# A written issue table for VectorE, ScalarE, GpSimd and the load queue, from the ninth MLA step to the fourth Strassen block

## The chip, the cores and the metric

The kernel runs on one core of one Trainium2 chip. Its time is the device time of one execution in microseconds (us). The engines are TensorE (PE; its weight loader is listed as PEld), VectorE (DVE), ScalarE (ACT), GpSimd (POOL) and SyncE (SP), which issues most of the DMAs. [...]

## The reference

One layer of a hybrid encoder block, with 512 tokens, 1024 features and float32 throughout:

```python
h = rms_norm(x);  z = h @ w_in                      # all latents, q, k, v
y_mla  = mla_group(...)                             # 8 heads, qk 96 wide, v 64
y_diff = diff_group(...)                            # 4 heads, two softmaxes of 64 each, v 128
x = x + concat([y_mla, y_diff]) @ w_out
h2 = rms_norm(x)
x = x + (silu(causal_conv3(h2 @ w_gate)) * (h2 @ w_up)) @ w_down     # 2816 wide
x = x + sigmoid(rms_norm(x) @ w_pg) * (p @ w_pp)
```

Attention is block-causal in chunks of 64, so of four blocks of 128 queries the block t looks at (t + 1) * 128 keys.

## The kernel before, in words

**Three products for one.** Every large product is made of three TensorE products (`mm3`, L154 to L159): high part by high part, high by low, low by high. So each weight tile of 128x1024 and each activation half of 128x512 is split first: ScalarE casts it to the high part (`hi_d`, `hi_o`, `wAh`, `wSh`, `wTh`, `b1h`, `yh`, `st`, `ah`), and VectorE subtracts that from the source to get the low part (`lo_o`, `wAl`, `yh1l`, `al`; L151, L186, L189, L957). Until both parts are there, TensorE can't begin the products that read them.

**The stages of the stretch.** The program is one long sequence without a loop on the chip.

- MLA steps: four pairs of heads (hp) by four query blocks (t), `i = 4*hp + t`. A step makes logits on TensorE (`ml`), their row maximum on VectorE (L587, L590), the exponentials on ScalarE (`mla_exp`, L605), the division by the sums on VectorE (`mla_norm`, L614), transposes on TensorE (`pTm`, L547), a copy of the transposed tile out of PSUM on either engine (`probs_T`, L550 and L552), and the product with v (`mo`, L635). `pump` puts products of another stage (z columns `zd`, later `o`) between these steps, as filling for TensorE.
- Differential steps: four heads by four query blocks. Per step two logits (`dl`), their bias and row minimum on VectorE (L735), exponentials (L736), the combination of the two softmaxes (`diff_comb`, L744 to L746), transposes `pTd`, a ScalarE copy `pt` (L550) and the product `do` (L754). `diff_T` transposes q and k of the next head and splits them into `st` (L185 to L189). When a head is done, ScalarE squares and copies its result (`sqo` L760, `yd` L761). The filling is W_out: `hi_o` and `lo_o` split its tiles, the products go to `o`, and VectorE adds them to x (`add_x`, L684).
- The start of the feed-forward part: squares of x (L1008) and their sums on VectorE and GpSimd (L1010, L1012), the norm (`nr`, L1051), the products with w_pp (`pp`), which ScalarE copies out of PSUM (`ppo`, L1066) and SP stores (`pps`), the normed halves `xg` and their casts `b1h`, `b2h`.
- Feed-forward blocks of 128 gate and 128 up columns: three plain ones, then blocks by Strassen's seven products (`gu_units`), whose half-width products `gx` ScalarE copies out of PSUM (L1198 to L1214), with sums of weight quarters on VectorE. `cv` is the convolution, `ah` and `al` its split result for W_down.

**What sets the order.** TensorE's order is as written, in one region over the whole program. VectorE, ScalarE and GpSimd have regions of their own (`tc.manual_schedule`), in which they too issue as the code is written: the first from the start to the second call of `diff_comb` (the end of the MLA steps), the second from the start of the feed-forward part to the fourth Strassen block. Between the two, over the differential steps and W_out, a scheduler places their instructions by its own estimates, bounded by holds such as `tc.issue_after(df["comb"].ins)`, which keep an instruction behind a named one. SP's order is the scheduler's throughout.

Of the kernel before, what the change touches and what calls it, by code (L numbers as in the profile page):

```python
# [15 lines left out]
ALU = mybir.AluOpType  # L16
# [47 lines left out]

UP_BANKS = ("lg", "tp", "tp", "ob")

def _bucket(rel):
# [20 lines left out]
def _f32(ap):  # L90
    return ap.bitcast(F32)
# [3 lines left out]
def hybrid_block(ctx: ExitStack, tc: tile.TileContext, a: dict, out: bass.AP):  # L95
    nc = tc.nc
    V, S, G, TE = nc.vector, nc.scalar, nc.gpsimd, nc.tensor
# [13 lines left out]
    def bank(tag, name):  # L111
        return pp_.tile([P, 512], F32, tag=tag, bufs={"acc": 2, "lg": 3, "tp": 2, "ob": 1}[tag], name=name)

    def tt(name, dtype=F32):
        return att.tile([P, T], dtype, tag="tt", bufs=16, name=name)
# [10 lines left out]
    def xn_tile(name):  # L126
        return keep.tile([P, D], F32, tag="xn", bufs=4, name=name)
# [4 lines left out]
    def th_tile(name):  # L132
        return wts.tile([P, T], F32R, tag="th", bufs=8, name=name), wts.tile([P, T], F32R, tag="tl", bufs=8, name=name + "l")
# [6 lines left out]
    def load_raw(src, n, name):  # L140
        raw = wp["rawpool"].tile([P, 1024], F32, tag="raw", bufs=wp["raw"], name=f"raw_{name}")
        nc.sync.dma_start(raw[:, :n], src)
        return raw

    def load_w(src, n, name, eng=None):

        raw = load_raw(src, n, name)
        hi = wp["pool"].tile([P, 1024], F32R, tag="hi", bufs=wp["w"], name=f"hi_{name}")
        lo = wp["pool"].tile([P, 1024], F32R, tag="lo", bufs=wp["w"], name=f"lo_{name}")
        S.copy(hi[:, :n], raw[:, :n])  # L150
        (eng or V).tensor_tensor(lo[:, :n], raw[:, :n], _f32(hi[:, :n]), op=ALU.subtract)  # L151
        return hi, lo

    def mm3(ps, blocks, first=True, last=True, again=False):  # L154
        n = len(blocks)
        for i, (xh, xl, wh, wl) in enumerate(blocks):
            TE.matmul(ps, xh, wh, start=first and i == 0, stop=False, skip_group_check=again)  # L157
            TE.matmul(ps, xh, wl, start=False, stop=False, skip_group_check=again)  # L158
            TE.matmul(ps, xl, wh, start=False, stop=last and i == n - 1, skip_group_check=again)  # L159
# [22 lines left out]
    def split(h_, l_, src, col=None, eng=None):  # L182

        if col is None:
            S.copy(h_, src)  # L185
            return (eng or V).tensor_tensor(l_, src, _f32(h_), op=ALU.subtract)  # L186
        else:
            S.activation(h_, src, AF.Identity, scale=col)
            return V.scalar_tensor_tensor(l_, src, col, _f32(h_), op0=ALU.mult, op1=ALU.subtract)  # L189

    tsl = [slice(t * P, (t + 1) * P) for t in range(NT)]

# [24 lines left out]
    region = tc.manual_schedule(engines={mybir.EngineType.DVE, mybir.EngineType.Activation, mybir.EngineType.Pool})  # L217
# [32 lines left out]
    for kq in range(4):  # L250
        raw = xn_tile(f"xT{kq}")
# [11 lines left out]
        for j in range(2):  # L263
            k = 2 * kq + j
            xs, ws = raw[:, j * T:j * T + T], slice(416 * j, 416 * j + 416)
            h_, l_ = th_tile(f"xh{k}")
# [60 lines left out]
    raw, ukv_ = load_raw(a["w_ukv"], 1024, "ukv"), []  # L327
    for c in range(2):
        h_, l_ = tt(f"ukvh{c}", F32R), tt(f"ukvl{c}", F32R)
# [70 lines left out]
    def z_flush():  # L400
        while zouts:
            zouts.pop(0)()
# [258 lines left out]
    yh, yl, df = [None] * 8, [None] * 8, {}  # L661
# [12 lines left out]
    def wo_blocks(k0, k1, b, w):  # L674

        c = [slice((k % 4) * 256 + (b % 2) * P, (k % 4) * 256 + (b % 2) * P + P) for k in range(k0, k1)]
        return [(w[0][:, c[i]], w[1][:, c[i]], yh[k0 + i], yl[k0 + i]) for i in range(k1 - k0)]
# [5 lines left out]
    def add_x(b, ps):  # L683
        V.tensor_tensor(xb(b), xb(b), ps, op=ALU.add)  # L684

    wo2, wo_first = {}, {}

    def wo_w(kq, dq):
        if (kq, dq) in wo_first:
            return wo_first.pop((kq, dq))  # L690
        return load_w(a["w_out"][kq, dq], 1024, f"o{kq}{dq}")

    def wo_units(kq, dqs, nk):

        for dq in dqs:
            w = wo_w(kq, dq)
            if kq == 0 and dq + 1 in dqs:
                with tc.issue_after(df["comb"].ins):
                    wo_first[0, dq + 1] = wo_w(0, dq + 1)
            if kq:  # L700
                wo2[dq] = w
            steps = [(b, k) for b in (2 * dq, 2 * dq + 1) for k in range(0, nk, 2)]
            if (kq, dq) == (0, 0):
                steps.sort(key=lambda s: s[1])
            ps = {}
            for b, k in steps:
                if k == 0:
                    ps[b] = bank("acc", f"o{kq}{b}")
                mm3(ps[b], wo_blocks(4 * kq + k, 4 * kq + k + 2, b, w), k == 0, k == nk - 2)
                if k == nk - 2:  # L710
                    add_x(b, ps[b])
                yield
# [130 lines left out]
    for hp in range(HP):  # L843
        for t in range(NT):
            i = NT * hp + t
            last = hp == HP - 1
            n = FILL_MLA[hp][t]
            if t:
                mla_norm(hp, t)
            if t < NT - 1:  # L850
                mla_logits(hp, t + 1)
            if t == 2:
                for c, (d, m) in enumerate(((diff_T, (0, 0)), (diff_T, (0, 1))) if last else ((mla_q, (2 * hp + 2,)), (mla_k, (2 * hp + 2,)))):
                    d(*m)
                    mla_exp(hp, t + 1, c)
            elif t < 2:
                for c in range(2):
                    mla_exp(hp, t + 1, c)
            else:
                pump()  # L860
                n -= 1
                if last:
                    diff_logits(0, 0)
                else:
                    mla_q(2 * hp + 3)
                    mla_k(2 * hp + 3)
            if t == 0:
                mla_norm(hp, t)
            for e in extra.get(i, ()):
                e()  # L870
            pump(n)
            for e in late.get(i, ()):
                e()
            mla_T(hp, t)
            z_flush()
            if i in pvs:
                mla_pv(*pvs[i])
            if t == 3 and not last:
                mla_logits(hp + 1, 0)
                for c in range(2):  # L880
                    mla_exp(hp + 1, 0, c)
# [6 lines left out]
    diff_T(1, 1)  # L888
    y_hl(2, ymn[2])
    diff_comb(0, 1)  # L890
    region.__exit__(None, None, None)
    pump()
    for i, (h, t) in enumerate(dslots):
        if i + 2 < len(dslots):
# [27 lines left out]
    pk = kvp.tile([P, 4, 1024], F32R, tag="kv", name="pk")  # L922
    for i, (src, name) in enumerate(((a["pT"], "pT"), (a["w_pp"][0], "pp0"))):
        raw = load_raw(src, 1024, name)
        S.copy(pk[:, 2 * i], raw)
        with tc.issue_after(df["scale"].ins):
            V.tensor_tensor(pk[:, 2 * i + 1], raw, _f32(pk[:, 2 * i]), op=ALU.subtract)
    ptw, wpp = (pk[:, 0], pk[:, 1]), [(pk[:, 2], pk[:, 3])]
    order = (0, 4, 1, 5, 2, 6, 3, 7)
    early = {}  # L930
# [32 lines left out]
    def behind_head(src, tag, name, bufs=1):  # L963

        h_, l_ = (ffn.tile([P, 1024], F32R, tag=tag + j, bufs=bufs, name=f"{tag}{j}{name}") for j in "hl")
        with tc.issue_after(df["copy"].ins):
            df["hi"] = S.copy(h_, src)
        with tc.issue_after(df["scale"].ins):
            df["lo"] = V.tensor_tensor(l_, src, _f32(h_), op=ALU.subtract)
        return h_, l_  # L970

    gu = lambda f, c0, c1: a["w_gu"][f][:, 512 * c0:512 * c1]
# [1 line left out]
    W = {0: {0: behind_head(raw_w(gu(0, 0, 2), "rA", 0, bufs=2), "wA", 0, bufs=2)}}  # L974
    wpp.append(behind_head(rpp, "wT", "pp1"))

    region = tc.manual_schedule(engines={mybir.EngineType.DVE, mybir.EngineType.Activation, mybir.EngineType.Pool})
    region.__enter__()
    nr_ = [ffn.tile([P, 1024], F32, tag="raw", bufs=2, name=f"nr{i}") for i in range(2)]
    nrm = {"ss": nr_[0][:, :T], "dg": nr_[0][:, T:], "r": nr_[1][:, :T]}  # L980

# [32 lines left out]
            V.tensor_tensor(nrm["ss"], nrm["ss"], half, op=ALU.add)  # L1014
            V.tensor_tensor(nrm["ss"], nrm["ss"], sq, op=ALU.add)

    held = ExitStack()
    for i in ("hi", "lo"):
        held.enter_context(tc.issue_after(df[i].ins))
    for b in order:  # L1020
        if b in early:
            ps = early[b]
            mm3(ps, wo_blocks(7, 8, b, wo2[b // 2]), False, True)
        else:
            ps = bank("tp" if b == 3 else "lg", f"o3{b}")
            mm3(ps, wo_blocks(6 if b < 4 else 4, 8, b, wo2[b // 2]), True, True)
        add_x(b, ps)
        sums_of(b)
        held.close()
    wts.release()  # L1030


# [335 lines left out]
    next(w5)  # L1368
    fill.append(down_units(*groups[0], range(2), dn0))
    next(g)  # L1370
    region.__exit__(None, None, None)
    held = tc.issue_after(W["last"].ins)
    held.__enter__()
    for _ in w5:
# [3 lines left out]
    for f in range(NPLAIN + 2, NF):  # L1378
# [13 lines left out]
        else:  # L1392
# [4 lines left out]
            for n, i in (("b1", 0), ("b2", 2)):  # L1397
                h_, l_ = (ffn2.tile([P, 2, 1024], F32R, tag=n + j, name=f"pg{n}{j}") for j in "hl")
# [58 lines left out]
    def pg_bank(b):  # L1457
        return bank("acc" if b % 4 < 2 else "tp", f"pg{b}")
# [26 lines left out]
    for b in range(4, NK - 1):  # L1485
        p = pg_bank(b)
        pg(b, p)
        ple_out(b, p)
    for c in (0, H2):
        p = pg_bank(NK - 1)  # L1490
# [81 lines left out]
```

## Time and profile before

| | |
|---|---|
| time, median of 3 runs | 641.84 us (641.34, 641.84, 641.89) |
| time of the profiled execution | 642.33 us |
| its span, first to last instruction | 640.6 us |
| mean granted TensorE clock | 0.998 |
| MLA logits `ml` on TensorE, first and last start | 70.4 to 143.1 us |
| differential logits `dl`, likewise | 150.1 to 205.4 us |
| W_out products `o`, likewise | 155.2 to 230.9 us |
| Strassen products `gx`, likewise | 276.4 to 543.6 us |

The profiled execution took 0.49 us more than the median of the runs, and 1.7 us of its time lie outside the span. Rows of the timeline have the start and the duration in us, the engine, the line, the operation, output and inputs, the shape; in square brackets stands how long the engine was idle ahead of the instruction and what released it. Rows of waits have the waiting instruction, what it waited for, the sum in us, how often, and the longest. A row with x3 at its end joins three instructions.

### The profile page before, as it was taken

How to read it: one execution, taken by the hardware profiler on the slowest of the kernel's cores; microseconds unless marked ns; L12 is line 12 of the kernel's file. 1: busy time of each engine (PE TensorE's matmuls, PEld its weight loads, DVE VectorE, ACT ScalarE, POOL GpSimd, SP SyncE). 2: the span in 40 equal slices, each digit the busy share in tenths (PEclk: the TensorE clock that was granted, in tenths of full speed). 3: DMA queues.
4: the chain of work that ended last, by engine and by line, in shares of the span. 5: the costliest groups of instructions: out<-in, count | busy, mean ns of one | idle time of the engine just before them, and what ended most of it. 6: DMA issues, size and time to landing. Idle time of an engine off the chain costs nothing.

```text
span 640.6 us, 10207 instructions
## 1 busy us (share of the span) xinstructions
PE 630.7 (98%) x3900; PEld 557.3 (87%) x3900; DVE 486.4 (76%) x870; ACT 360.0 (56%) x629; POOL 68.5 (11%) x94
## 2 busy tenths in 40 slices
PE   9999999999999999999999999999999999999997
PEld 9988888886777887889999999999999999988886
DVE  6889677887899678888976767676767676759844
ACT  7896476756667455656554554545454545637111
POOL 1524103030000140101000000010000000000000
PEclk9999999999999999999999999999999999999999
DMA  8351611330231447547865646564646453542021
GB/s 294 112 165 33 187 66 62 100 131 2 67 100 34 164 135 243 133 99 166 215 186 123 194 119 181 116 181 116 182 115 184 119 175 116 182 131 64 31 87 50
DMA packets 29912, 82.63 MB, mean 129 GB/s; under 512 B 3100, under 2 KB 4124, under 8 KB 29736
## 3 DMA queue, kind: packets, MB, share of 16 engines
q1 hardware_dynamic: 23816, 69.17, 32.7%
q0 software_dynamic: 5616, 12.33, 11.3%
q8 instruction: 31, 0.51, 0.3%
q10 hardware_dynamic: 432, 0.49, 0.2%
q14 instruction: 17, 0.14, 0.1%
HBM read 77.77 MB, written 5.52 MB: 130 GB/s over the span
## 4 chain that ended last, share of the span: by engine, by line
PE 86%; DVE 7%; ACT 3%; issue 2%; DMA 1%; ACTq 0%; DVEq 0%; SPq 0%
PE dn L157 6%; PE dn L158 6%; PE dn L159 6%; PE gx L159 4%; PE gx L158 4%; PE gx L157 4%; PE zd L157 3%; PE zd L159 3%; PE zd L158 3%; PE g L157 3%; PE g L158 3%; PE g L159 3%; PE pg L159 2%; PE pg L158 2%; PE pg L157 2%
## 5 line engine op out<-in xcount | busy, mean ns | idle before, releaser
L957 DVE TENSOR_TENSOR wSl<-rS,wSh 128x1024 fp32r<-128x1024 f32 x21 | 25.7, 1224 | 43.6 <-ACT wSh L953 43.4
L157 PE MATMUL dn<-ah,hi_dn 128*128 128x512 f32 x144 | 56.2, 391 | 0.0
L158 PE MATMUL dn<-al,hi_dn 128*128 128x512 f32 x144 | 56.2, 391 | 0.0
L159 PE MATMUL dn<-ah,lo_dn 128*128 128x512 f32 x144 | 56.0, 389 | 0.0
L1074 POOL DMA_DIRECT2D rS<-in_w_gu x19 | 22.7, 1194 | 250.1 <-DVE cv L1242 115.2
L953 ACT CAST wSh<-rS 128x1024 fp32r<-128x1024 f32 x21 | 22.0, 1047 | 35.9 <-PE gy L158 35.6
L157 PE MATMUL zd<-hi_d,xh 128*128 128x512 f32 x96 | 39.2, 409 | 0.0
L158 PE MATMUL zd<-lo_d,xh 128*128 128x512 f32 x96 | 37.5, 391 | 0.0
L957 DVE TENSOR_TENSOR wTl<-rA,wTh 128x1024 fp32r<-128x1024 f32 x19 | 23.3, 1225 | 15.2 <-ACT wTh L953 14.7
L684 DVE TENSOR_TENSOR x<-x,dn 128x512 f32<-128x512 f32 x44 | 29.8, 678 | 6.1 <-PE dn L159 6.1
L159 PEld LDWEIGHTS dn<-ah,lo_dn 128*128 128x128 f32 x144 | 27.0, 188 | 5.7
L157 PEld LDWEIGHTS dn<-ah,hi_dn 128*128 128x128 f32 x144 | 27.1, 188 | 5.1
L158 PEld LDWEIGHTS dn<-al,hi_dn 128*128 128x128 f32 x144 | 27.1, 188 | 5.0
L1245 ACT ACTIVATE cv<-cv 128x512 f32<-128x512 f32 x22 | 13.9, 630 | 23.9 <-DVE cv L1242 23.8
L957 DVE TENSOR_TENSOR wAl<-rA,wAh 128x1024 fp32r<-128x1024 f32 x21 | 25.5, 1217 | 2.2 <-ACT wAh L953 2.2
L157 PE MATMUL o<-yh,hi_o 128*128 128x512 f32 x64 | 26.8, 419 | 0.0
L157 PE MATMUL g<-b2h,wAh 128*128 128x256 f32 (+1 forms) x88 | 26.4, 300 | 0.4 <-ACT g L1198 0.2
L953 ACT CAST wAh<-rA 128x1024 fp32r<-128x1024 f32 x21 | 22.1, 1050 | 8.3 <-DMA rA<-in_w_gu 8.2
L158 PE MATMUL g<-b2l,wAh 128*128 128x256 f32 (+1 forms) x88 | 26.2, 297 | 0.0
L159 PE MATMUL g<-b2h,wAl 128*128 128x256 f32 (+1 forms) x88 | 26.2, 297 | 0.0
L736 ACT ACTIVATE pmd<-pmd,nmd 128x128 f32<-128x128 f32 (+3 forms) x32 | 17.9, 560 | 14.7 <-DVE nmd L735 14.7
L1465 ACT ACTIVATE sg<-sg 128x512 f32<-128x512 f32 (+1 forms) x9 | 5.3, 584 | 36.8 <-DVE sg L1464 36.8
(479 smaller groups left out, 2219.6 us busy)
## 6 DMA issues: line engine op xcount, KB each, us to landing
rA<-in_w_gu SPq DMA_DIRECT2D x22, 512.0 KB, 3.9
rS<-in_w_gu SPq DMA_DIRECT2D x22, 512.0 KB, 3.7
rS<-in_w_gu POOLq DMA_DIRECT2D x19, 512.0 KB, 6.1
raw_dn<-in_w_down SPq DMA_DIRECT2D x18, 512.0 KB, 5.8
raw_d<-in_w_d SPq DMA_DIRECT2D x12, 512.0 KB, 3.4
r<-in_w_gu SPq DMA_DIRECT2D x19, 256.0 KB, 5.9
raw_o<-in_w_out SPq DMA_DIRECT2D x8, 512.0 KB, 3.7
rS_pg<-in_w_pg SPq DMA_DIRECT2D x6, 512.0 KB, 4.0
```

Source lines behind the costliest of these rows:

```text
L157: TE.matmul(ps, xh, wh, start=first and i == 0, stop=False, skip_group_check=again)
L158: TE.matmul(ps, xh, wl, start=False, stop=False, skip_group_check=again)
L159: TE.matmul(ps, xl, wh, start=False, stop=last and i == n - 1, skip_group_check=again)
L684: V.tensor_tensor(xb(b), xb(b), ps, op=ALU.add)
L736: S.activation(pm[:, :n], pm[:, :n], AF.Exp, bias=nm, scale=-1.0, accum_out=s0 if m == 0 else s1)
L953: S.copy(h_, src)
L957: V.tensor_tensor(l_, src, _f32(h_), op=ALU.subtract)
L1074: nc.gpsimd.dma_start(sums[f].rearrange("p (i c) -> p i c", i=2), a["w_gu"][f][:, :2048].rearrange("p (i c) -> p i c", i=2)[:, :, :512], a ...
L1245: S.activation(cv, cv, AF.Silu)
L1465: S.activation(sg, sg, AF.Sigmoid)
```

## The change

TensorE's region stays as it is. The first region of the other engines now ends at the ninth MLA step (`i == 8`), where the position in the program is marked; the second region and all holds between are gone. At the place where the second region ended, `in_order(mark)` takes all instructions of VectorE (305), ScalarE (191), GpSimd (14) and SP (42) since the mark and chains each engine's in the order of a written table. Each link only orders two instructions of the same engine; no semaphore comes with it.

```diff
+ISSUE = {
+    mybir.EngineType.DVE: [
+        0, 7, 1, 2, 3, 4, 5, 8, 6, 36, 9, 10, 12, 11, 13, 14, 15, 17, 27, 28, 18, 19, 21, 23, 22, 24, 20, 25, 26, 16, 31, 33, 30, 37, 32, 47, 34, 35,
...
+    mybir.EngineType.SP: [
+        0, 5, 6, 7, 1, 2, 3, 4, 8, 9, 10, 11, 12, 13, 14, 15, 16, 20, 26, 27, 28, 34, 17, 18, 19, 29, 31, 21, 36, 22, 23, 24, 25, 39, 30, 33, 32, 37,
+        35, 40, 38, 41,
+    ],
+}
...
+    def traced():
+        return len(nc.cur_bb.bb.instructions)
+
+    def in_order(mark):
+
+        ins = nc.cur_bb.bb.instructions
+        for e, order in ISSUE.items():
+            x = [i for i in ins[:mark] if i.engine == e and type(i).__name__.startswith("Inst")][-1:]
+            y = [i for i in ins[mark:] if i.engine == e and type(i).__name__.startswith("Inst")]
+            assert sorted(order) == list(range(len(y)))
+            x += [y[k] for k in order]
+            for p, q in zip(x, x[1:]):
+                tc.add_manual_dep(q, p.name, mybir.DependencyInfo(mybir.DependencyClass.NoSync, mybir.DependencyReason.DATA), reason="issue order")
...
-                with tc.issue_after(df["comb"].ins):
-                    wo_first[0, dq + 1] = wo_w(0, dq + 1)
+                wo_first[0, dq + 1] = wo_w(0, dq + 1)
...
+            if i == 8:
+                region.__exit__(None, None, None)
+                mark = traced()
...
     diff_comb(0, 1)
-    region.__exit__(None, None, None)
...
-    region = tc.manual_schedule(engines={mybir.EngineType.DVE, mybir.EngineType.Activation, mybir.EngineType.Pool})
-    region.__enter__()
...
     next(g)
-    region.__exit__(None, None, None)
+    in_order(mark)
```

The left-out hunks remove the other holds (`df["copy"]`, `df["scale"]`, `df["hi"]`, `df["lo"]`). Both programs hold the same instructions with the same shapes and tiles; TensorE's 3760 and GpSimd's 99 rows stand in the same order in both. SP has two moves among its 164: one load of `rS` and one of the 128x512 weight tile `r` now each stand ahead of a load for W_down. The rest of the change is the order on VectorE and ScalarE. In the listings below a number behind a name marks one tile; tiles made later in the program have numbers lower by one or two after the change, and lines of the changed kernel are 32 to 46 higher.

VectorE at the turn from the MLA steps to the differential ones: `dl` are the first differential logits, `pTm` the last transposed MLA tiles, `yh1l` the low part of an MLA result, which only W_out reads. Before:

```order
L552 COPY pt<-pTm_1732 128x384
L613 RECIPROCAL sums<-sums 128x2
L614 TENSOR_SCALAR pm<-pm,sums 128x512 x2
L735 ISA pmd,nmd<-dl_1764,strip 128x128
L735 ISA nmd 128x1
L735 ISA pmd,nmd<-dl_1772,strip 128x128
L735 ISA nmd 128x1
L186 TENSOR_TENSOR yh1l<-ym_1425,yh_1780 128x512
L552 COPY pt<-pTm_1784 128x512
```

The same place after:

```order
L218 TENSOR_TENSOR yh1l<-ym_1426,yh_1781 128x512
L598 COPY pt<-pTm_1733 128x384
L659 RECIPROCAL sums<-sums 128x2
L660 TENSOR_SCALAR pm<-pm,sums 128x512 x2
L780 ISA pmd,nmd<-dl_1765,strip 128x128
L780 ISA nmd 128x1
L183 TENSOR_TENSOR lo_o_1973<-raw_o_1970,hi_o_1972 128x1024
L598 COPY pt<-pTm_1785 128x512
L780 ISA pmd,nmd<-dl_1773,strip 128x128
```

`yh1l` has moved from right ahead of the copy of `pTm_1784` to six rows earlier; in its place, two rows up, stands a low part of W_out, `lo_o`, and the copy has passed the second logits' `L735`.

ScalarE where the first differential head ends and the third one's q is split (`d0T_2083` into `st`). Before:

```order
L736 ACTIVATE pmd,s_1948<-pmd,nmd 128x384
L736 ACTIVATE pmd,s_2036<-pmd,nmd 128x384
L550 COPY pt<-pTd_2064 128x128
L150 CAST hi_o_2504<-raw_o_2502 128x1024
L760 ACTIVATE sqo<-do_1946 128x512
L761 COPY yd_2072<-do_1946 128x512
L188 ACTIVATE st<-d0T_2083,dcol 128x512
L736 ACTIVATE pmd,s_1948<-pmd,nmd 128x512
```

The same place after:

```order
L596 COPY pt<-pTd_2064 128x128
L781 ACTIVATE pmd,s_1948<-pmd,nmd 128x384
L805 ACTIVATE sqo<-do_1946 128x512
L806 COPY yd_2072<-do_1946 128x512
L220 ACTIVATE st<-d0T_2083,dcol 128x512
L781 ACTIVATE pmd,s_2036<-pmd,nmd 128x384
```

The cast `hi_o_2504` has gone from here. It now stands a whole step earlier on ScalarE, ahead of another copy of transposed probabilities:

```order
L781 ACTIVATE pmd,s_1867<-pmd,nmd 128x384
L182 CAST hi_o_2504<-raw_o_2502 128x1024
L596 COPY pt<-pTd_1941 128x256
L781 ACTIVATE pmd,s_1763<-pmd,nmd 128x512
L781 ACTIVATE pmd,s_1913<-pmd,nmd 128x512
```

ScalarE in the first Strassen blocks: the copy of `gx_3113` (3111 after) frees the PSUM bank for the next product. Before:

```order
L953 CAST wAh_3043<-rA_3041 128x1024
L1130 ACTIVATE bth<-xg_2851 128x512
L1131 CAST bth<-xg_2873 128x512
L953 CAST wTh_3059<-rA_3041 128x1024
L185 CAST ah_3063<-cv 128x512
L1198 COPY g_3114<-gx_3113 128x256
```

The same place after:

```order
L999 CAST wAh_3041<-rA_3039 128x1024
L1169 CAST bth<-xg_2856 128x512
L217 CAST ah_3020<-cv 128x512
L1169 CAST bth<-xg_2871 128x512
L999 CAST wTh_3057<-rA_3039 128x1024
L999 CAST wAh_3136<-rA_3134 128x1024
L1236 COPY g_3112<-gx_3111 128x256
```

The 128x512 cast of the convolution's result `ah_3063` (3061 after) has gone from ahead of the copy, and the next block's weight cast `wAh_3136` has come there.

More of the change, by code (lines that the diff above doesn't have):

```diff
@@ L65 @@
 UP_BANKS = ("lg", "tp", "tp", "ob")
+ISSUE = {
+    mybir.EngineType.DVE: [
[11 rows of a table added]
+    ],
+    mybir.EngineType.Activation: [
[6 rows of a table added]
+    ],
+    mybir.EngineType.Pool: [
+        0, 1, 2, 3, 4, 5, 6, 7, 8, 9, 10, 11, 12, 13,
+    ],
+    mybir.EngineType.SP: [
+        0, 5, 6, 7, 1, 2, 3, 4, 8, 9, 10, 11, 12, 13, 14, 15, 16, 20, 26, 27, 28, 34, 17, 18, 19, 29, 31, 21, 36, 22, 23, 24, 25, 39, 30, 33, 32, 37,
+        35, 40, 38, 41,
+    ],
+}
 def _bucket(rel):
@@ L925, in hybrid_block @@
         S.copy(pk[:, 2 * i], raw)
-        with tc.issue_after(df["scale"].ins):
-            V.tensor_tensor(pk[:, 2 * i + 1], raw, _f32(pk[:, 2 * i]), op=ALU.subtract)
+        V.tensor_tensor(pk[:, 2 * i + 1], raw, _f32(pk[:, 2 * i]), op=ALU.subtract)
     ptw, wpp = (pk[:, 0], pk[:, 1]), [(pk[:, 2], pk[:, 3])]
@@ L965, in behind_head @@
         h_, l_ = (ffn.tile([P, 1024], F32R, tag=tag + j, bufs=bufs, name=f"{tag}{j}{name}") for j in "hl")
[L966 to L969, printed above, removed]
+        S.copy(h_, src)
+        V.tensor_tensor(l_, src, _f32(h_), op=ALU.subtract)
         return h_, l_
@@ L1015, in sums_of @@
             V.tensor_tensor(nrm["ss"], nrm["ss"], sq, op=ALU.add)
-    held = ExitStack()
-    for i in ("hi", "lo"):
-        held.enter_context(tc.issue_after(df[i].ins))
     for b in order:
@@ L1028, in hybrid_block @@
         sums_of(b)
-        held.close()
     wts.release()
```

16 rows, old and new, of the table ISSUE are left out of this document.

## The prediction

> **What bounds the kernel now.** I read the page first, its span:
>
> ```profile
> span 640.6 us, 10207 instructions
> ```
>
> and the chain of work that ended last, by engine:
>
> ```profile
> PE 86%; DVE 7%; ACT 3%; issue 2%; DMA 1%; ACTq 0%; DVEq 0%; SPq 0%
> ```
>
> TensorE carries the chain. So the kernel gets shorter only where TensorE stands still, and the next view is the busy time by stretch: the stretch of the change, rounded outward, and the steady blocks behind it.
>
> ```profile
> 130.00:300.00 170.00, 165.84 (x992) 136.99 (x991) 139.02 (x295) 102.56 (x209) 18.70 (x13) 1.00 0.40 118
> 300.00:500.00 200.00, 200.00 (x1390) 187.54 (x1389) 148.77 (x202) 104.83 (x158) 16.68 (x14) 1.00 0.60 158
> ```
>
> The columns are length, then busy time of PE, PEld, DVE, ACT and POOL, then granted clock. From 130 to 300 us TensorE idles 170.00 - 165.84 = 4.16 us; from 300 to 500 us never. What the change wins before 300 us is therefore not given back by a queue behind it: TensorE is the bound there, and it only starts earlier. What TensorE waited for in the stretch, and three rows of its weight loader's waits that the first list does not have in full:
>
> ```profile
> PE mo L635 <- DVE pt L552: 0.7, 1, 0.7
> PE pTm L547 <- DVE pm L614: 0.6, 1, 0.6
> PE dl L159 <- DVE st L189: 0.6, 1, 0.6
> PE pTm L547 <- DVE st L186: 0.5, 1, 0.5
> PE g L157 <- ACT ppo L1066: 0.5, 1, 0.5
> PE pTd L547 <- ACT pt L550: 0.5, 1, 0.5
> PE g L157 <- ACT g L1198: 0.2, 1, 0.2
> ```
>
> ```profile
> PEld g L157 <- ACT g L1198: 1.0, 2, 0.7
> ...
> PEld gx L159 <- DVE wAl L957: 0.5, 2, 0.3
> ...
> PEld dl L157 <- ACT st L188: 0.3, 1, 0.3
> ```
>
> The seven waits make 3.6 us. They understate the loss, because a product's last part overlaps its follower: in the rows of 278.78 and 279.01 us below, products that are listed with 0.39 us start 0.23 us apart, so a stall costs its listed idle time and 0.16 us more. From below a wait costs its listed idle time, from above that and 0.16.
>
> **The change part by part.** TensorE's instructions, order and shapes are the same, so no work is added or removed on it. What changes is when the other engines' results come. I go through the listed waits.
>
> *pTm behind pm (0.6).* The division waits for row maxima that VectorE takes late:
>
> ```profile
> 134.41 0.28 PE L159 MATMUL ml<-st 100*128 100x128 f32 x1
> ```
>
> ```profile
> 135.08 0.41 DVE L590 TENSOR_REDUCE sums<-ml 128x2 f32<-128x256 f32 x1
> ```
>
> The logits end at 134.41 + 0.28 = 134.69, the maximum starts 0.39 later, behind two scalings of `zd` and a copy. In the table one of the two scalings has left that place. Gain at most 0.39 and at least 0; I take 0.30, as some hand-over remains. The remaining 0.3 or so of this wait is the chain itself.
>
> *pTm behind st (0.5).*
>
> ```profile
> 145.30 0.74 DVE L189 SCALAR_TENSOR_TENSOR st<-d0T,dcol,st 128x512 fp32r<-128x512 f32 x1
> ...
> 146.44 0.69 DVE L186 TENSOR_TENSOR st<-d1T,st 128x512 fp32r<-128x512 f32 x1 [0.40 <-ACT st L185]
> ```
>
> The second split waits 0.40 for a ScalarE cast, which stood behind an exponential there. The table puts both casts ahead of the exponentials and takes a reduction from between the two VectorE splits, so the second follows the first at about 145.96 (145.30 + 0.74, less the 0.08 by which such operations overlap): 0.48 earlier. The bounds are 0.4 (the idle time shown) and 0.5 + 0.16; I take 0.48.
>
> *mo behind pt (0.7).*
>
> ```profile
> 152.39 0.69 DVE L186 TENSOR_TENSOR yh1l<-ym,yh 128x512 fp32r<-128x512 f32 x1 [1.24 <-ACT yh L185]
> 153.00 0.68 DVE L552 COPY pt<-pTm 128x512 f32<-128x512 f32 x1
> ```
>
> `yh1l`, wanted only by W_out, held the copy back for 153.00 - 152.39 = 0.61. It moves away; in its place comes a `lo_o`, 1.22 long by its like at 197.06 below, but ahead of it VectorE idled 1.24. Gain 0.60; 0 if that `lo_o` starts late, 0.87 (0.7 + 0.16) if the copy may start earlier still. I take 0.60, since the 1.24 covers the 1.22 with nothing to spare.
>
> *dl behind st (0.6, and the loader's 0.3).* ScalarE ran a weight cast in front of the evictions of a finished head and the split behind them:
>
> ```profile
> 174.79 1.05 ACT L150 CAST hi_o<-raw_o 128x1024 fp32r<-128x1024 f32 x1
> ```
>
> Lost are 0.6 + 0.16 at this wait and, by the loader's row, 0.3 at the `dl` that waits for ScalarE's half: 1.0. The cast of 1.05 goes from this chain, and VectorE makes the low half of `st` one logit earlier. Gain 1.0; from below 0.6, the wait shown.
>
> *pTd behind pt (0.5).*
>
> ```profile
> 197.06 1.22 DVE L151 TENSOR_TENSOR lo_o<-raw_o,hi_o 128x1024 fp32r<-128x1024 f32 x1
> ```
>
> ```profile
> 199.94 0.40 ACT L736 ACTIVATE pmd<-pmd,nmd 128x128 f32<-128x128 f32 x1 [1.89 <-DVE nmd L735]
> ```
>
> ScalarE stood 1.89 for a VectorE minimum behind that `lo_o`, then did this exponential, then the copy. The table moves the `lo_o` behind other work and this exponential ahead of an earlier copy. Gain 0.55, between 0.40 (the exponential alone) and 0.66 (0.5 + 0.16).
>
> *g behind ppo (0.5).*
>
> ```profile
> 240.36 0.59 ACT L1051 COPY nr<-nrb 128x512 f32<-128x512 f32 x1 [2.98 <-PE nrb L1050]
> ...
> 244.33 0.58 ACT L1066 COPY ppo<-pp 128x512 f32<-128x512 f32 x1
> ```
>
> Lost: 0.5 + 0.16 = 0.66, behind the copy of 244.33, which like two others ran between the casts of the normed halves. Two of these copies move into the 2.98 us in which ScalarE had nothing to do. Gain 0.66, and 0 if the chain from the norm to the casts is late itself.
>
> *g behind g, gx behind wAl (0.2 in the first list, 1.0 and 0.5 in the loader's).*
>
> ```profile
> 277.75 1.05 ACT L953 CAST wTh<-rA 128x1024 fp32r<-128x1024 f32 x1
> 278.71 0.61 ACT L185 CAST ah<-cv 128x512 fp32r<-128x512 f32 x1
> 279.22 0.36 ACT L1198 COPY g<-gx 128x256 f32<-128x256 f32 x1
> ```
>
> ```profile
> 278.78 0.39 PE L158 MATMUL u<-b2l,wSh 128*128 128x512 f32 x1
> 279.01 0.39 PE L159 MATMUL u<-b2h,wSl 128*128 128x512 f32 x1
> 279.64 0.39 PE L157 MATMUL g<-b2h,wAh 128*128 128x256 f32 x1 [0.24 <-ACT g L1198]
> ```
>
> Lost here: 0.63 - 0.23 = 0.40; the like of it some 18 us later 0.3 (the loader's 1.0 less its longest, 0.7). The table takes `ah` away and sets `wTh` and the next `wAh` so far ahead that ScalarE waits for TensorE at the copy. The two `wAl` move right behind `wTl`: 0.4 of the loader's 0.5. Gain 0.40 + 0.3 + 0.4 = 1.1.
>
> [...]
>
> **What the moves cost.** Ten 1024-wide pieces of W_out (four `hi_o` at 1.05, six `lo_o` at 1.22, by their rows above; 11.5 us in all) stand at other places of the differential steps, among them three `hi_o` right in front of copies of `pTd`. ScalarE is busy 102.55 of 170.00 us, so mostly they fall into idle time; from below 0, from above three times 1.05. I take 0.5, half of one cast, since the stalls shown behind such a piece (0.6 behind the `hi_o` of 1.05, 0.5 behind the `lo_o` of 1.22) were about half of it.
>
> At the start of the feed-forward part a load is held back:
>
> ```profile
> 226.02 3.07 DVE L684 TENSOR_TENSOR x<-x,o 128x512 f32<-128x512 f32 x5
> ```
>
> ```profile
> 226.55 0.38 SPq L948 DMA_DIRECT2D r<-in_w_gu  x1
> ```
>
> ```profile
> r<-in_w_gu SPq DMA_DIRECT2D x19, 256.0 KB, 5.9
> ```
>
> SP's next `rS` load waits until VectorE has made w_pp's low part, which the table puts behind the additions to x: these end at 229.09, the low part (1.22) at 230.3, the load of `r` behind it goes out near 231.2 instead of 226.55 and lands 5.9 later, near 237.1. Its cast now stands between the second and third `ppo`, so ScalarE and all behind it wait for it; then three copies of some 0.5 end near 239.3, 1.1 ahead of the `nr` copy at 240.36. So I cost it at nothing; a landing over 1.1 us later would come through. The other load that SP takes earlier, ahead of one for W_down, has a consumer far behind the stretch and costs nothing.
>
> GpSimd's sums of squares now run beside w_pp's low part, whose two inputs lie in SBUF. The nearest row is a VectorE sum of two SBUF inputs that fell into a GpSimd sum:
>
> ```profile
> 227.44 4.38 POOL L1010 TENSOR_TENSOR nr<-nr,nsq 128x512 f32<-128x512 f32 x3 [9.90 <-ACT nsq L1008]
> ```
>
> ```profile
> 229.85 0.82 DVE L1012 TENSOR_TENSOR nr<-nr,nsq 128x512 f32<-128x512 f32 x1 [0.76 <-ACT nsq L1008]
> ```
>
> It took 0.82 against 0.69 for `yh1l` of the same shape at 152.39: 0.13 more. So I cost the overlap at 0.1, which lies off the path and adds nothing to the sum; bounds 0 and one GpSimd sum, 4.38 / 3 = 1.46. [...]
>
> **The sum.** 0.30 + 0.48 + 0.60 + 1.0 + 0.55 + 0.66 + 1.1 = 4.7, less 0.5 for new waits: 4.2. Against its own time the profiled execution would take 642.33 - 4.2 = 638.1; the median lies 0.49 below the profiled run, 641.84 - 4.2 = 637.6, say 637.7.
>
> **The rivals.**
> - *Half is given back.* A freed TensorE asks for everything earlier, and some results then come too late: a `hi_o` in front of a `pTd` copy shows in full at two of three places (2.1), or the overlap with GpSimd or the late `r` delays the norm (1.0 to 1.5). For it: the `lo_o` that replaces `yh1l` fits by 0.02 us. Against it: ScalarE and VectorE have 67 and 31 us idle between 130 and 300 us. Time: half the gain, 641.84 - 2.1 = 639.7.
> - *Nothing moves.* The waits sit in chains (logit, maximum, exponential, sum, division, transpose, copy) that are as long in any order, and each place that is eased shows the next engine's lateness. For it: two releasers are VectorE, two ScalarE in the same chains. Against it: the rows show at each place one instruction that isn't of the chain. Time 641.8.
> - *Slower.* One mechanism: the moved 1024-wide splits in the differential steps come to stand in front of `pTd` copies and minima that TensorE waits for. They hold 11.5 us; more than 4.7 + 1.3 = 6.0 of it, over half, must show on TensorE before the kernel is slower by 0.2%. With 7 it would take 641.84 + 7 - 4.7 = 644.1. Against it: before, the same ten were there as well, and cost some 1.5 (1.0 at `dl`, 0.55 at `pTd`).
>
> **How the numbers follow.** My forecast has 0.66, half given back 0.22, nothing 0.08, slower 0.04. The forecast's own ends are 636.7 (no new wait, 4.7, and 0.4 from the upper ends of the first and third place) and 638.9 (a sum of 2.9: the lower ends of the terms for `st`, `dl` and `pTd`, 0.4 + 0.6 + 0.40, in place of 2.03, and a whole cast shown, 1.05, and 0.1 of the overlap with GpSimd). The range takes in half given back with some more: 636.7 to 640.3. What a measurement of this kernel can tell from no change is about 0.2%, 1.3 us. Faster by more than that holds the first two cases: 0.88; within it 0.08; slower 0.04.
>
> **What would show it.** Right: in the changed kernel TensorE idles at most 1.5 us between 130 and 300 us, the waits for `st`, `pt` of L552, `ppo` and `g` are gone from its list, and each stage starts earlier by the sum so far (half a microsecond less from the `hi_o` on): the first `dl` by 0.8, the first plain block's `g` by 3.1, the steady blocks by 4.2 us. Wrong: a wait of `do` or `pTd` for `pt` behind a `hi_o`; `nr` no earlier than before; a gap ahead of the first `g` behind `r`; or idle time behind 300 us, since the order at the end of the stretch hands over to the scheduler.

## The result

The changed kernel takes 636.25 us (median of 6 runs, 635.92 to 637.34) against 641.95 us (6 runs, 641.34 to 643.64): a ratio of 0.991, 95% interval 0.9896 to 0.9923, or 5.7 us. Forecast were 637.7 and a range of 636.7 to 640.3, so it gained more than was forecast, and 0.45 us more than the range allowed. Its profiled execution took 635.92 us, 0.33 below its median. Of all runs reported here one, of the kernel with the new order in the second half only, took 1251.71 us; it is left out of that kernel's median.

The span and the chain that ended last, from the page of the changed kernel:

```profile
span 634.2 us, 10212 instructions
...
PE 98%; DMA 1%; DVE 1%; ACT 0%; issue 0%; ACTq 0%
```

VectorE and ScalarE, 10% of the chain before, have all but left it. The same two stretches as before (length, then busy time of PE, PEld, DVE, ACT and POOL), and all waits of TensorE that are listed in the first:

```profile
130.00:300.00 170.00, 169.37 (x1021) 141.39 (x1020) 143.55 (x302) 108.27 (x215) 16.91 (x13) 1.00 0.43 127
300.00:500.00 200.00, 200.00 (x1397) 187.90 (x1396) 145.46 (x197) 103.64 (x155) 15.50 (x13) 1.00 0.58 154
```

```profile
PE pTm L593 <- DVE pm L660: 0.3, 1, 0.3
PE mo L681 <- DVE pt L598: 0.2, 1, 0.2
```

TensorE idles 0.63 us where it idled 4.16, and of seven waits two are left. For `pm` the prediction had named a rest of 0.3; the one for `pt` (L552 before) it had expected to be gone, and 0.2 of it is left. Behind 300 us it still never idles.

TensorE issues the same products in the same order in both kernels, so one product's start before, less its start after, is the advance won up to there. The two profiled executions differ by 0.67 us already at 60 us, and still at 120 us; the first moved instruction runs at 114 us. That part is no effect of the change and is taken off here.

| product | start before | start after | advance, less 0.67 | step | the prediction's term |
|---|---|---|---|---|---|
| `pTm` behind `pm` | 137.43 | 136.43 | 0.33 | 0.33 | 0.30 |
| `pTm` behind `st` | 147.19 | 145.60 | 0.92 | 0.59 | 0.48 |
| `mo` behind `pt` | 153.74 | 151.64 | 1.43 | 0.51 | 0.60 |
| `dl`, third head, last product of the pair | 178.73 | 175.35 | 2.71 | 1.28 | 1.0 |
| `dl`, fourth head, last product of the pair | 195.39 | 191.73 | 2.99 | 0.28 | none |
| `pTd` behind `pt` | 200.85 | 196.67 | 3.51 | 0.52 | 0.55 |
| first `g` of the feed-forward part | 244.97 | 240.07 | 4.23 | 0.72 | 0.66 |
| second `g` product behind `gx`'s copy | 279.86 | 274.48 | 4.71 | 0.48 | 0.40 |
| `gx` product after that behind `wAl` | 283.27 | 277.60 | 5.00 | 0.29 | 0.2 |
| second `g` product of the next block | 298.30 | 291.89 | 5.74 | 0.74 | 0.5 |
| new waits | | | | 0 | -0.5 |

The steps make 5.74, and the medians differ by 5.70. The row of 279.86 holds three things: the wait for `gx`'s copy, 0.48; 0.16 more won at the products right behind the first `g`; and a loss of 0.17 at the second half of the first plain block, where a copy of `pp` stood 1.8 us behind a store. That loss is in this profile alone; the profiles of all runs below lack it, and without it the sum would be 5.9.

### The profile page after: what moved, and what is told of

Read it like the earlier page. It is cut to its first block, busy times and chain, and to the rows that moved or that the text cites. A ratio compares the mean times of both kernels' runs of the same rounds, so it can differ in the third digit from the quotient of the medians.

```text
span 634.2 us, 10212 instructions
## 1 busy us (share of the span) xinstructions
PE 627.6 (99%) x3900; PEld 555.7 (88%) x3900; DVE 485.3 (77%) x870; ACT 360.7 (57%) x629; POOL 69.7 (11%) x94
## 3 DMA queue, kind: packets, MB, share of 16 engines
q0 software_dynamic: 5616, 12.33, 11.5%
## 4 chain that ended last, share of the span: by engine, by line
PE 98%; DMA 1%; DVE 1%; ACT 0%; issue 0%; ACTq 0%
PE dn L189 6%; PE dn L190 6%; PE dn L191 6%; PE gx L191 4%; PE gx L190 4%; PE gx L189 4%; PE g L190 4%; PE g L191 4%; PE g L189 4%; PE zd L189 4%; PE zd L191 3%; PE zd L190 3%; PE o L189 3%; PE o L191 2%; PE u L189 2%; PE o L190 2%
## 5 line engine op out<-in xcount | busy, mean ns | idle before, releaser
L999 ACT CAST wTh<-rA 128x1024 fp32r<-128x1024 f32 x19 | 20.0, 1050 | 11.9 <-PE g L190 9.3
```

## The experiments

All edit the table of the changed kernel only. A number in it is an instruction's place in the code as written, counted from the mark; "ahead" and "behind" are on one engine. Advances are read as in the table above, from 120 us on.

**Is it the order alone, and do its parts add?** First the old order, written as a table:

```diff
-    mybir.EngineType.DVE: [0, 7, 1, 2, 3, 4, 5, 8, 6, 36, ...
+    mybir.EngineType.DVE: [0, 1, 2, 3, 4, 5, 6, 7, 8, 9, ...
-    mybir.EngineType.Activation: [2, 0, 1, 7, ...       # likewise
```

> The changed program, but the table lists the order that each engine had before; regions and holds stay removed. Theory A (the order alone makes the gain): 641.3 to 642.6 us, and from 130 to 300 us TensorE waits at the same places as before, 3.6 us listed. Rival C (a part of the 5.7 us comes from the removed regions and holds or from how the table is enforced, not from the order): 640.5 or less.

641.94 us, ratio to before 0.9995 (0.9982 to 1.0009). By the start times it is 0.14 us behind before at 300 us. One row of its stretches:

```profile
130.00:300.00 170.00, 165.70 (x993) 136.94 (x992) 138.84 (x295) 103.16 (x210) 18.28 (x14) 1.00 0.40 118
```

4.30 us idle, where it was 4.16, and the seven waits of before are back. In its trace VectorE, ScalarE, GpSimd and SP run in the order that they had before. So taking away regions and holds, and enforcing a table, are worth nothing that can be measured; the order is the whole change.

Then the new order in one half and the old in the other, cut at the squares of x (ScalarE's 117, VectorE's 205):

```diff
+    DVE: [new order of 0..204] + [205, 206, 207, ... as before]
+    Activation: [new order of 0..116] + [117, 118, ... as before]
```

> The table's new order up to the end of W_out, the old order from the squares of x on. Theory A (the places add, and the advance is kept): 3.5 us of the 5.7, 638.4 us, within 0.5; TensorE starts the last W_out product 3.5 us earlier and loses nothing of it later. Rival B (as the prediction sized it: attention 2.9 less 0.5 for casts in front of copies): 2.4, 639.5.

> The old order up to the end of W_out, the table's new order from the squares of x on. Theory A: 2.2 us of the 5.7, 639.7 us, within 0.5; 0.7 of it at the first plain block's first product, 1.5 in the first two Strassen blocks. Rival B (as the prediction sized it, 0.66 and 1.1): 1.8, 640.2; the traces tell these two apart, by the start times of TensorE's products.

The first took 639.08 us, ratio 0.995 (0.993 to 0.997), the second 639.70 (five runs), 0.9956 (0.9938 to 0.9973); the kernel before, timed beside them, took 642.47. What TensorE still waits for from 130 to 300 us, in the first and in the second:

```profile
PE g L190 <- ACT ppo L1105: 0.5, 1, 0.5
PE g L190 <- ACT g L1237: 0.5, 2, 0.4
PE pTm L594 <- DVE pm L661: 0.3, 1, 0.3
PE mo L682 <- DVE pt L599: 0.2, 1, 0.2
```

```profile
PE mo L682 <- DVE pt L599: 0.7, 1, 0.7
PE pTm L594 <- DVE pm L661: 0.6, 1, 0.6
PE dl L192 <- DVE st L222: 0.6, 1, 0.6
PE pTm L594 <- DVE st L219: 0.6, 1, 0.6
PE pTd L594 <- ACT pt L597: 0.5, 1, 0.5
```

Each half has lost its own waits and kept the other's; only that for `g` is longer in the first, 0.5 for 0.2. The times can't tell theory A from rival B in either case; the start times can. The advance is 3.55 us at 240 us in the first and 3.29 at 300, so 0.26 of it is lost again in the half with the old order. In the second it is 0.17 and 2.55, so 2.38 for its half. 3.55 + 2.38 = 5.93 against 5.74 together: they add, to some tenths. Of the 0.7 and 1.5 expected of the second half, 0.86 and 1.52 came.

**Did the casts in front of copies cost the 0.5?** The three `hi_o` go right behind the copies that they preceded:

```diff
-        97, 48, ... 104, 52, ... 110, 77,
+        48, 97, ... 52, 104, ... 77, 110,
```

> The changed kernel with the three hi_o casts that stand right ahead of copies of pTd (hi_o10, hi_o11, hi_o12) moved right behind these copies. Theory A (ScalarE runs the casts while it would wait for the transposes): TensorE's starts stay within 0.1 us of the changed kernel's, or get later. Rival B (the prediction's 0.5 for new waits): TensorE is up to 0.5 us earlier from there on.

635.84 us in one run, and TensorE's starts stay within 0.04 us up to 240 us. ScalarE at the second of the three places, in the changed kernel and then here:

```profile
161.27 1.05 ACT L182 CAST hi_o<-raw_o 128x1024 fp32r<-128x1024 f32 x1 [0.65 <-PE o L190]
162.22 0.37 ACT L596 COPY pt<-pTd 128x256 f32<-128x256 f32 x1
```

```profile
161.81 0.37 ACT L597 COPY pt<-pTd 128x256 f32<-128x256 f32 x1 [0.17 <-PE pTd L594]
162.08 1.05 ACT L183 CAST hi_o<-raw_o 128x1024 fp32r<-128x1024 f32 x1
```

The copy comes 0.4 us earlier and TensorE doesn't: nothing was waiting for it. The three casts, by which the term of 0.5 was priced, cost nothing. The moved `lo_o` were not tried by themselves, but of the two waits left in the list above none stands behind one.

**What does one wait cost?** A weight cast ahead of the copy of `gx`, then two:

```diff
-        161, 165, 163,
+        161, 165, 166, 163,          # one cast: wSh3
+        161, 165, 166, 183, 163,     # two: wSh3, hi_dn001
```

> The changed kernel with the weight cast of 1.05 us for the first Strassen block (wSh3) ahead of the copy of gx that it now follows. The cast waits for TensorE's last plain product, so the copy ends about 1.5 us after TensorE wants it. Theory A (restart): from start to start TensorE loses the listed idle time and 0.26: 0.16 at the first product and 0.10 at the second. Rival B (the prediction's rule): the listed idle time and 0.16, with the second product 0.12 behind the first.

> The changed kernel with two casts of 1.05 us (hi_dn001 and wSh3) ahead of the copy of gx, where one cost a listed wait of 1.22 us. If the first can run while ScalarE waits for TensorE anyway, the wait is the same 1.2 us and the loss 1.5; if it comes behind the other's wait, 2.2 us and 2.4. Theory A: the loss is the listed wait and 0.26, whatever its length, with the clock at 1.00. Rival D (a wait of 1.8 us or more can bring the clock down): some microseconds at a clock of 0.50 and 2 to 3 us more, where the wait is that long.

With one cast 637.73 us, with two 638.58 (one run each). TensorE with one, then with two:

```profile
274.44 0.39 PE L192 MATMUL u<-b2h,wSl 128*128 128x512 f32 x1
276.06 0.39 PE L190 MATMUL g<-b2h,wAh 128*128 128x256 f32 x1 [1.22 <-ACT g L1237]
276.28 0.28 PE L191 MATMUL g<-b2l,wAh 128*128 128x256 f32 x1
```

```profile
274.38 0.39 PE L192 MATMUL u<-b2h,wSl 128*128 128x512 f32 x1
276.94 0.39 PE L190 MATMUL g<-b2h,wAh 128*128 128x256 f32 x1 [2.17 <-ACT g L1237]
277.16 0.28 PE L191 MATMUL g<-b2l,wAh 128*128 128x256 f32 x1
```

With one cast: 276.06 - 274.44 = 1.62, less the pace of 0.23, is 1.39 = 1.22 + 0.17; and the second product stands 0.22 behind the first instead of 0.12. Together 1.49, and the start times of everything behind are 1.50 later. With two: 2.17 + 0.16 + 0.10 = 2.43, measured 2.42. So the price of a wait ahead of 256-column products is its listed idle time and about 0.26, at both lengths.

**What does a late half of `st` cost?** VectorE's low half of the fourth head's q goes behind the second minimum and an addition:

```diff
-        148, 153, 155, 159, 161,
+        148, 155, 159, 153, 161,
```

> The changed kernel with VectorE's low half of the fourth head's q moved behind the second minimum and one addition to x, so that it ends near 191.8 us, when TensorE wants it near 191.73. Theory A (pairs): a wait too short to be listed, 0 to 0.3 us, still breaks the pair of logits, and from that place on TensorE is 0.3 to 0.6 us later than in the changed kernel. Rival B (only the wait counts): 0 to 0.3 later, and the six products of the pair still take 0.28 from the first start to the last.

637.0 us in one run. The same products in the changed kernel (rows with x2 hold two products that start together) and here:

```profile
191.45 0.33 PE L189 MATMUL dl<-st 64*128 64x128 f32 x2
191.62 0.28 PE L190 MATMUL dl<-st 64*128 64x128 f32 x2
191.73 0.28 PE L191 MATMUL dl<-st 64*128 64x128 f32 x2
```

```profile
191.66 0.32 PE L190 MATMUL dl<-st 64*128 64x128 f32 x1
191.83 0.27 PE L191 MATMUL dl<-st 64*128 64x128 f32 x1
192.73 0.32 PE L192 MATMUL dl<-st 64*128 64x128 f32 x1 [0.63 <-DVE st L222]
192.74 0.32 PE L190 MATMUL dl<-st 64*128 64x128 f32 x1
192.90 0.27 PE L191 MATMUL dl<-st 64*128 64x128 f32 x1
193.01 0.27 PE L192 MATMUL dl<-st 64*128 64x128 f32 x1
```

The two logits of a step use 64 rows each and run side by side; a wait in the first keeps the second back until it is over. The wait was longer than expected, since the addition itself waited for TensorE: 0.90 from start to start less 0.11 is 0.79, and the second logit then takes 0.27 by itself. TensorE is 1.06 later from there on. The total missed its expectation of 0.3 to 0.6; the price of the pair, 0.27, came as expected. That a wait too short to be listed parts a pair too, this run no longer tests; the profiles of the old order do, further down.

The third head's place was undone too, with the VectorE half alone and with the cast `hi_o11` as well. The second of these kernels ran first, so the first one's expectation names its result:

```diff
-        123, 122, 116, 121, 117, 118, 124,         # VectorE, both kernels
+        123, 116, 121, 117, 118, 124, 122,
-        104, 52, ... 63, 61,                       # ScalarE, the second kernel
+        52, ... 63, 104, 61,
```

> The changed kernel with VectorE's low half of the third head's q behind the second logit's minimum; the cast hi_o11 stays away. Theory A: a listed wait of about 1.2 us, and TensorE later by that and 0.16 and 0.27 for the pair, 1.6 in all; the granted clock stays at 1.00 behind it. Rival D (the drop of the clock behind the wait of 1.82 us in the other kernel comes from the place, not from the wait's length): the clock falls to 0.50 here too, and 2 to 3 us more are lost.

> The changed kernel with one place undone: the cast hi_o11 again ahead of the evictions of the first differential head, and VectorE's low half of the third head's q again behind the second logit's minimum. Theory A: the low half comes about 1.5 us after the first of the two logits wants it, and the two logits, which now run side by side, go one behind the other, which costs 0.27 more: 1.6 to 1.9 us in all, 637.9 to 638.1, with the six products of the pair spread over more than the wait. Rival B: the listed wait and 0.16 only, as the prediction counted it; the pair takes no longer than in the changed kernel once the wait is over.

The VectorE half alone: 637.75 us in one run, and by the start times 1.65 later: 1.24 + 0.16 + 0.27 = 1.67.

```profile
177.13 0.32 PE L192 MATMUL dl<-st 64*128 64x128 f32 x1 [1.24 <-DVE st L222]
177.14 0.33 PE L190 MATMUL dl<-st 64*128 64x128 f32 x1
```

With the cast as well the expectation missed: 640.01 us (638.31 to 642.03 over 10 runs), ratio to before 0.9965 (0.995 to 0.9979), and in its profile TensorE is 5.3 us later, not 1.6 to 1.9. Its products, and its stretches (the third number from the end is the granted clock):

```profile
177.79 0.47 PE L192 MATMUL dl<-st 64*128 64x128 f32 x1 [1.82 <-DVE st L222]
177.80 0.47 PE L190 MATMUL dl<-st 64*128 64x128 f32 x1
```

```profile
177.00:178.00 1.00, 0.20 (x2) 0.21 (x3) 1.00 (x4) 0.81 (x2) 0.00 (x0) 0.81 0.00 0
178.00:184.00 6.00, 6.00 (x17) 4.62 (x18) 3.70 (x11) 0.00 (x0) 0.00 (x0) 0.50 0.16 45
184.00:186.00 2.00, 2.00 (x18) 1.73 (x16) 0.00 (x0) 0.90 (x2) 0.00 (x0) 0.89 0.35 135
```

A mean of 0.81 over the first microsecond is 0.38 us at half the clock, and 0.89 over the last two are 0.44, so the clock was 0.50 from 177.62 to 184.44 us, 6.8 us: it fell inside the wait, 0.17 us ahead of its end. The wait, the overlap and the pair make 1.82 + 0.16 + 0.27 = 2.25; the other 3.0 are these 6.8 us. The mean clock of its runs goes from 0.993 to 0.999, and the run at 0.999 took 638.31, which is 2.1 us above the changed kernel's median: by this one run, the price of the place without the drop.

The kernel with two casts waits longer, 2.17 us, and showed no drop. It was timed again for that:

> The same kernel as the one with two casts ahead of the copy of gx, now timed several times for its clock. Theory E (whether a wait of about 2 us brings the clock down is a matter of its moment, so it varies from run to run): 638.5 us where the mean clock is 0.998 or more, and some runs 2 to 3 us longer with a mean clock of 0.997 or less. Rival F (the drop belongs to the differential step alone): all runs within 638.2 to 639.5 with a clock of 0.998 or more.

639.01 us (638.46 to 640.01, 5 runs), ratio to before 0.9952 (0.9937 to 0.9967); the clock was 0.998 or more in four runs and 0.997 in the one of 640.01, and its new profile shows the same 2.42 us and 1.00 throughout that place. So the length of a wait alone doesn't bring the clock down: it fell in the one of 1.82 us and in neither profile of the longer one. The run of 640.01 lies outside rival F's range; theory E is not settled by five runs, and what makes the difference is open.

**Does the overlap with GpSimd cost anything?** w_pp's low part goes ahead of the additions to x again:

```diff
-        203, 205, 206, 207, 208, 209, 210, 204, 212,
+        203, 204, 205, 206, 207, 208, 209, 210, 212,
```

> The changed kernel with the low part of w_pp's second tile ahead of the additions to x again, so that it doesn't run beside GpSimd's sums. Theory A (the two share something, in part, off TensorE's path): that operation falls from 1.87 to 1.22 us, the norm sum that took 1.18 to 0.7 to 0.9, and TensorE's start of the first plain block stays within 0.1 us. Rival B (the overlap costs time on the path): the norm and TensorE's first plain product come 0.3 us or more earlier.

636.33 us in one run. VectorE and GpSimd in the changed kernel, then here:

```profile
223.54 1.30 POOL L1052 TENSOR_TENSOR nr<-nr,nsq 128x512 f32<-128x512 f32 x1
...
224.06 1.87 DVE L1013 TENSOR_TENSOR wTlpp<-rS_pp,wThpp 128x1024 fp32r<-128x1024 f32 x1
...
224.93 2.16 POOL L1052 TENSOR_TENSOR nr<-nr,nsq 128x512 f32<-128x512 f32 x1
...
226.45 1.18 DVE L1054 TENSOR_TENSOR nr<-nr,nsq 128x512 f32<-128x512 f32 x1
```

```profile
220.68 1.22 DVE L1014 TENSOR_TENSOR wTlpp<-rS_pp,wThpp 128x1024 fp32r<-128x1024 f32 x1
...
226.24 0.82 DVE L1055 TENSOR_TENSOR nr<-nr,nsq 128x512 f32<-128x512 f32 x1
...
226.59 1.61 POOL L1053 TENSOR_TENSOR nr<-nr,nsq 128x512 f32<-128x512 f32 x1
```

The overlap costs VectorE 0.65 and 0.36 and GpSimd's last sum 0.55, and TensorE nothing: its starts stay within 0.05 us up to 240 us.

The rows show more: here the two engines took turns. In the changed kernel GpSimd's sum ends at 223.54 + 1.30 = 224.84, and VectorE's operation, begun at 224.06, ends 1.09 after that, at 225.93. GpSimd's next sum, begun at 224.93, ends 1.16 after VectorE's, at 227.09; VectorE's sum, begun at 226.45, ends 0.54 after that, at 227.63. Undisturbed, these take 1.22, 1.30 and 0.69. So each of these three, which came second, ended its own length, less 0.13 to 0.15, after the other's end: it waited for all that was left of the other. The 0.82 above is such a wait as well, for the last 0.27 us of a GpSimd sum.

**Is there more to have?** Two swaps on ScalarE, where the changed kernel's trace shows copies in the way:

```diff
-        106, 107, ... 138, 139, 141,
+        107, 106, ... 139, 141, 138,
```

> The changed kernel with two swaps on ScalarE: the seventh copy of pp behind the next two casts b2h instead of ahead of them, where it waited 1.78 us for a store, and the last copy of pTd (512 columns) ahead of the high part yh6. Theory A (each place is worth what TensorE loses there): 0.17 to 0.25 at the second half of the first plain block and 0.15 to 0.3 at the last product of the differential part, together 0.3 to 0.55 by the start times; in the time 635.7 to 636.0, which the runs can hardly tell from 636.25. Rival B (another wait takes the place): 0.1 or less.

636.21 us, ratio to before 0.9909 (0.9891 to 0.9926): the same as the changed kernel. The first swap lost 0.29, since `yh6` now ends later and the W_out products that read it wait:

```profile
208.92 0.58 ACT L597 COPY pt<-pTd 128x512 f32<-128x512 f32 x1 [0.84 <-PE pTd L594]
209.40 0.69 ACT L221 ACTIVATE yh<-yT,ocol 128x512 fp32r<-128x512 f32 x1
```

At the second the start times are 0.19 better than in the changed kernel's profile, but so they are in the profiles of all other runs, which don't have this swap: the wait behind the store is in that one profile only. Nothing was won.

## Why the prediction was wrong

What held: TensorE's waits are the whole of it, the advance is kept to the end (the halves add, and 300 to 500 us stays without idle time), and the forecast's places are the ones that went. TensorE idles 0.63 us where at most 1.5 were forecast. Half given back, no change and slower did not come.

Two steps of the sum failed, in the same direction, and both made the forecast too small.

- **"Less 0.5 for new waits."** It measured nothing: the casts in front of the `pTd` copies cost no start time of TensorE, by the run that moves them behind. The argument for half a cast came from places where ScalarE had been late already. Here it would have idled at 161 us, and TensorE had filling to do.
- **"From below a wait costs its listed idle time, from above that and 0.16."** That upper end isn't one. The terms made 4.7, the places gave 5.74. Of the 1.05 between them, 0.55 is the pair of logits: 0.27 of the term `dl behind st`, and all of the fourth head's place, where a wait too short for the list parted the pair: six starts over 0.55 us before, from 194.84 to 195.39, and over 0.28 after. Another 0.4 is the second product behind a wait in the Strassen blocks, 0.10 late at each of four places. With both rules the sum before the 0.5 would have been 5.6. Each was there to be read before: the second `g` product in 279.86, 0.22 behind the first, and the `dl` at 178.45, two products that start together, then one logit by itself:

```profile
178.45 0.32 PE L159 MATMUL dl<-st 64*128 64x128 f32 x1 [0.57 <-DVE st L189]
178.45 0.32 PE L157 MATMUL dl<-st 64*128 64x128 f32 x1
178.61 0.27 PE L158 MATMUL dl<-st 64*128 64x128 f32 x1
178.73 0.27 PE L159 MATMUL dl<-st 64*128 64x128 f32 x1
...
194.84 0.32 PE L157 MATMUL dl<-st 64*128 64x128 f32 x1
...
195.11 0.32 PE L157 MATMUL dl<-st 64*128 64x128 f32 x1
...
195.39 0.27 PE L159 MATMUL dl<-st 64*128 64x128 f32 x1
```

The fourth head's 0.28 depends on the profile: with the old order put back in the table, the same six starts spread over 0.44 us, and with the old order in the first half only, over 0.30, with hardly anything lost. That is where the 0.17 comes from by which the second kernel is ahead at 240 us. So beside the changed kernel's 0.28 this place cost 0.27, 0.16 and 0.02 us in the three profiles.

The rest is a tenth here and there: `st` 0.59 for 0.48, `mo` 0.51 for 0.60, the first `g` 0.72 for 0.66. The range failed with them: its low end of 636.7 was made from 4.7 and 0.4 of margin, by bounds of each wait that left out what a wait does to the products behind it. The 0.4 took in the upper ends of two places only; those of `st` and `pTd`, 0.18 and 0.11, would have made it 636.4, still above the 636.25 measured. (The upper end for `mo`, 0.7 + 0.16, is 0.86 and not 0.87; nothing hangs on it.)

What was priced at nothing and was nothing: the held-back load of `r` let ScalarE wait 0.57 us for its cast, and the copies behind it were done in time.

```profile
231.44 0.62 ACT L999 CAST w22h<-r 128x512 fp32r<-128x512 f32 x1 [0.57 <-DMA r<-in_w_gu]
```

The GpSimd overlap was sized at 0.1 and took 0.65 at the larger operation, off the path as argued. The size failed because one row was read wrongly: its 0.13 was taken for the price of an overlap, while that VectorE sum, begun at 229.85 us, had only waited for the last 0.26 us of a GpSimd sum (228.82 + 1.29 = 230.11):

```profile
228.82 1.29 POOL L1010 TENSOR_TENSOR nr<-nr,nsq 128x512 f32<-128x512 f32 x1
```

In the changed kernel whoever came second waited for all that was left of the other, by the ends of 224.84, 225.93 and 227.09 us above. Of the 1.0 to 1.5 us by which the first rival has the norm delayed, the upper end is near the 1.46 of one GpSimd sum; no run shows the 1.0, nor any such loss: without the overlap TensorE's starts stay within 0.05 us up to 240 us.

The rival that ends slower was argued by how much of 11.5 us would have to show. The run with `hi_o11` put back shows how it could have come sooner: one place with a wait of 1.82 us cost up to 5.3.

## What to carry to other kernels

When a tuned kernel is bound by one engine, price a reorder by the bound engine's start times, from the last product ahead of a wait to the third or so behind it, and not by the list of waits: it leaves out short waits and everything that a wait does to its followers. A long instruction in front of an eviction cost nothing here, where its engine would have idled and the bound engine had filling; ask at each place, with the idle time in front of that row, instead of taking a share of its length. To know whether a mechanism or an order makes a gain, write the old order with the new mechanism.

## What the runs showed of the hardware

- Two products of 64 rows each that follow one another ran side by side (starts of 191.45, 191.62 and 191.73 us, two each), and waits of 0.57 to 1.24 us in the first put them one behind the other, for 0.27 us more. Where no wait was listed, at the fourth head before, they were parted as well: the six starts lie 0.55 us apart, against 0.28 after.
- A wait ahead of 256-column products cost about 0.26 us beside its listed time (1.22 listed, 1.50 lost; 2.17 listed, 2.42 lost).
- In a wait of 1.82 us the granted clock fell to 0.50, 1.65 us after TensorE's last product had ended (175.97 to 177.62 us), and stayed there for 6.8 us, which cost about 3 us. A wait of 1.24 us left it at a mean of 1.00 over its run, and one of 2.17 elsewhere at 1.00 throughout that place. What makes the difference, no run shows.
- A VectorE operation with two SBUF inputs and a GpSimd sum took turns, whoever came second waiting for the other's end: 1.87 us for 1.22 on VectorE, 2.16 for 1.30 on GpSimd, 1.18 for 0.69 on VectorE. VectorE's additions `x`, whose second input is in PSUM, took 0.68 or 0.69 beside the same sums.
